# A gate's row moved from the last product's sum on VectorE into that product's weights on GpSimd, in a hybrid attention and Fourier block

## The chip, the core and the metric

The kernel runs on 1 core of one Trainium2 chip. The profile calls the core's engines PE (TensorE, matrix products; PEld are its weight loads), DVE (VectorE), ACT (ScalarE), POOL (GpSimd) and SP (SyncE, which here only issues DMAs). A queue's name ends in q, so SPq and POOLq are DMAs issued by SP and by POOL. The metric is the device time of one execution in microseconds (us). Before the change the median of 3 runs is 1297.37 us (1297.19 to 1297.37).

## The reference, cut to what matters

One layer for 512 tokens with 2048 channels. The end of it is all that the change touches:

```python
def _merge(p_rest, attn, w_pa, w_pb, w_o):
    ...
    return (g_a * y_a + g_b * y_b) @ w_o          # 512 x 2048 by 2048 x 2048

    shift, scale, gate = jnp.split(silu_c @ w_ada[l] + b_ada[l], 3, axis=-1)
    ...
    y = _merge(p[..., OFF_ZA:], attn, w_proj_a[l], w_proj_b[l], w_out[l])
    new_xs = xs + gate[:, None] * y               # gate: one value for each channel
    ...
    return _rmsnorm(xs, final_g)                  # over the 2048 channels of a token
```

`gate` depends on the condition alone, so it is one row of 2048 numbers. A product's column c is multiplied by gate[c], which is the same as a product with weights whose column c was multiplied by gate[c] beforehand.

## The kernel before, in words

All products are f32, worked out as three fp32r products each: a factor is split into a high part (ACT copies it rounded, L179) and a low part (DVE subtracts, L180), and PE sums high*high, high*low and low*high (L335, L336, L337). Tiles `whi`, `wlo` and, in turn with them, pairs named `s` hold the split weights; a raw weight tile has 128 partitions x 1024 (two blocks of 128 rows by 512 columns) and is named `wr` (loaded by SP) or `R` (see below).

The large products are done by a scheme of seven half-size products in place of eight (Strassen and Winograd). A group is a product of 512 tokens by 2048 channels with 1024 output columns, of which two groups, 8 and 9, make the output projection `w_o`. In group 9, the last one of the kernel, the seven products run in the order P1, Q5, P2, Q6, P7, Q3, Q4. Each has 4 weight pieces and 48 matmuls. Products with a letter Q take weights that are sums of blocks of `w_o`: four tiles `R` (in this text the chain), one for each piece, are added to by DMAs from POOL (L288). For P7, DVE subtracts a freshly loaded block from the chain's tile to get P7's weights (L273), and then the last block is added to the chain, which gives Q4's weights. Q4's four pieces are split straight from the four tiles `R`.

The sums of the seven products lie in PSUM (`banks`) and are joined by DVE into tiles `X`, `V` and `Y` (L1085), each 2 x 512 columns for 128 tokens at a time. A finished quarter (its half of the tokens, and one of four ranges of 512 columns) is multiplied by the gate's row on DVE (L1839), and x is added to it by a DMA from POOL that accumulates in SBUF (L1841). In the last group this is turned round to save work at the end:

- `prepare` (L1803) forms x - gate*X before product P7 and x - gate*Y before product Q3, by one DVE instruction (L1806) and one accumulating DMA (L1807) each.
- Q4 is summed on in the same PSUM banks as P7, so that the banks hold P7+Q4 at the end. `finish` (L1136) runs Q4 for the first 128 of the half's tokens over all pieces (t = 0), then for the second 128 (t = 1), and calls `last` after each.
- `last` (L1886) multiplies the banks by the gate's row (L1894), adds that to x - gate*Y in two halves of 256 columns (L1896), sums the squares (ACT, L1791), and scales the four quarters of those tokens by the root mean square and the final row (L1879, L1881, L1867), each followed by its store (L1845, L1868).
- Before it, `out_done` for the quarter (0, 1), called when Q3 is done (L1809), does the same with L1814 and L1815 for the first half of the tokens, in an order on DVE and ACT that is written out by hand.

The order of the rest is set by a recording scheduler: `get` (L294) splits weights ahead of their use, as far as there are tiles for them, and in group 9 the split of a piece follows the split before it. A tile's readers wait by semaphores for its writers. Each engine's instructions, and the DMA issues among them, run in the order in which they stand.

`split_piece` (L261) is the place at which a weight piece is split. The rows of the gate lie in SBUF as `gates[0]` and `gates[1]` of 128 x 1024 each, the same values in all partitions, loaded by POOL (L1744).

Of the kernel before, what the change touches and what calls it, by code (L numbers as in the profile page):

```python
# [13 lines left out]
ALU = mybir.AluOpType  # L14
# [4 lines left out]
P = 128  # L19
# [52 lines left out]
def context_piece(g, name, pc):  # L72

    n = 28 * (g - NQZ) + 4 * ONE_GROUP.index(name) + pc
    if n % 2 == 0 and 0 <= n < 8:
        return "cn", n // 2
    if n % 7 == 4 and 18 <= n < 46:
        return "cr", n // 7 - 2
# [43 lines left out]
def block_kernel(ctx, tc, xT, ctx_rows, ctx_toks, x, c_row, w_ss, w_gate, vecs, qkg, rope, dft_c, dft_s,  # L122
                 w_start, w_g, w_pab, w_o, final_g, out):
    nc = tc.nc
# [30 lines left out]
    def uid(s):  # L155
        cnt[0] += 1
        return f"{s}{cnt[0]}"
# [20 lines left out]
    def split_from(src, hi, lo):  # L178
        first = nc.scalar.activation(hi, src, ACT.Copy)  # L179
        return first, nc.vector.tensor_tensor(lo, src, hi.bitcast(F32), op=ALU.subtract)  # L180
# [58 lines left out]
    def int_tiles(n):  # L239
        return [Halves([pairs[2 * n + k][i][:, :, 256:] for k in range(2)]) for i in range(2)]  # L240

    def hl_tiles():
        if more_hl and not more_hl[0]:
            hl_pools.extend(range(MORE_HL))
            more_hl.clear()
        elif more_hl:
            more_hl[0] -= 1
        hl_pools.append(hl_pools.pop(0))
        pool = hl_pools[-1]
        if isinstance(pool, tuple):  # L250
            return [slot_tile(p, (1024,), F32R) for p in pool]
        if isinstance(pool, int):
            return int_tiles(pool)
        return [pool.tile([P, 1024], F32R, tag=t, bufs=hl_pools.count(pool), name=uid("w" + t)) for t in ("hi", "lo")]
# [2 lines left out]
    last_split, split_of, in_line = [], [], []  # L257

    look = [1]

    def split_piece(e):  # L261
        if e.out is not None or e.kind == "raw":
            return
        raws = [r for _, r in e.raws]
        src = raws.pop(0) if e.stage is None else chain[e.pc]
        for r in raws:
            nc.vector.tensor_tensor(src, src, r, op=ALU.add)
        if e.off:
            with ExitStack() as line:
                if e.key[1] in DIFF_IN_LINE:  # L270

                    line.enter_context(tc.issue_after(split_of[-2][1].ins))
                nc.vector.tensor_tensor(src, chain[e.pc], src, op=ALU.subtract)  # L273
        hi, lo = e.dst() if e.dst else hl_tiles()
        if isinstance(hi, Halves):
            for k in range(2):
                last_split.append(split_from(src[:, 512 * k : 512 * k + 512].rearrange("p (a c) -> p a c", a=2),
                                             hi.parts[k], lo.parts[k]))
        else:
            hi, lo = hi[:, : e.cols], lo[:, : e.cols]  # L280
            with ExitStack() as line:
                if in_line:
                    for i in last_split[-1]:
                        line.enter_context(tc.issue_after(i.ins))
                last_split.append(split_from(src, hi, lo))
        split_of.append(last_split[-1])
        if e.nxt is not None:
            nc.gpsimd.dma_start(chain[e.pc], e.nxt, accum_op=ALU.add)  # L288
        if e.stage == 3:
            left[e.pc] = 0  # L290
        r = lambda t: t if isinstance(t, Halves) else t.rearrange("p (n m) -> p n m", n=e.n)
        e.out = (r(hi), r(lo))

    def get(key):  # L294
        load_more()
        turn = [e for e in ahead if not e.aside]
        assert turn[0].key == key, (turn[0].key, key)
        for e in turn[: min(look[0], len(hl_pools))]:
            if e is turn[0] or e.key[0] != "V":
                split_piece(e)  # L300
        load_more()
        e = turn[0]
        ahead.remove(e)
        free.extend(p[0::2] for p, _ in e.raws if p in retired)
        return e.raws[0][1] if e.kind == "raw" else e.out
# [14 lines left out]
    def slot_tile(p, shape, dt):  # L320
        return p[0].tile([P] + list(shape), dt, tag=p[1], bufs=1, name=uid("s"))

    def take(shape, dt=F32, pool=None):
        p = next((p for p in free if p[0] is pool), free[0])
        free.remove(p)
        t = slot_tile(p, shape, dt)
        home[id(t)] = p, t
        return t
# [89 lines left out]
    for g in range(LAST + 1):  # L418
        for name in ONE_GROUP:
# [6 lines left out]
            for pc in range(4):  # L426
                p = context_piece(g, name, pc)
                if p:
                    src, cols = (ctx_toks[p[1]], 1024) if p[0] == "cn" else (ctx_rows[p[1]], 4 * C)
                    stream(p, src, cols, 1, "raw")  # L430
                    todo.insert(len(todo) - 4 + pc, todo.pop())
            for pc in range(4):
                if (g, name, pc) in GATE_AT:
                    q = GATE_AT[g, name, pc]
                    stream(("gate", q), w_gate[q], 1024, 1, "raw")
                    e = todo.pop()
# [286 lines left out]
    def split_next():  # L723
        e = next(e for e in ahead if e.out is None and e.kind != "raw")
        split_piece(e)
        e.raws = []
# [27 lines left out]
    with tc.manual_schedule(engines={E.PE}):  # L754
# [6 lines left out]
        with tc.manual_schedule(engines={E.Activation, E.DVE}):  # L761
# [25 lines left out]
            for kb in range(1, 4):  # L787
                k = kb + 1
# [32 lines left out]
            for kb in range(4, KK - 4, 2):  # L821
# [6 lines left out]
                k = kb + 2  # L828
# [104 lines left out]
    for g in range(4):  # L933
        gate_b(g)
        positions(g)
        if g < 2:
            channels(g + 2)
        with behind((finals[-1], low[g])):
            for e in ahead[:g]:
                split_piece(e)  # L940
# [66 lines left out]
    def job():  # L1007
        tick[0] += 1
        due = next((x for x in later if x[0] <= tick[0]), None)
        if due:  # L1010
            later.remove(due)
            due[1]()
        elif jobs:
            jobs.pop(0)()
# [10 lines left out]
    class Group:  # L1025
# [110 lines left out]
        def finish(self, a, form):  # L1136

            w = []
            for t in range(2):
                for j in range(8):  # L1140
                    if len(w) <= j // 2:
                        w.append(get(("Q4", self.g, j // 2)))
                        job()
                        job()
                    self.mm(a, form, j, t, w[j // 2], False, j == 7, cont=True)
                self.last(self.Y, a, t)

    def gate_done(half, c, v, t):
# [498 lines left out]
    for i in range(NSTEP + 3):  # L1647
        h, t = divmod(i, 4)
# [29 lines left out]
        if i == 3:  # L1678
            with tc.issue_after(maxima[0].ins), tc.issue_after(maxima[1].ins):
                e = take((1024,))  # L1680
# [58 lines left out]
    gates, fgs = {}, {}  # L1739

    def load_rows(g):
        for l, src in ((gates, gs.rearrange("(o k) p -> o (k p)", o=1)), (fgs, final_g)):
            l[g] = take((2, 512))
            nc.gpsimd.dma_start(l[g], src[:, 1024 * g : 1024 * g + 1024].broadcast_to([P, 1024]))  # L1744
# [42 lines left out]
    new_o = lambda: take((2, 512))  # L1787
    squared = take((1024,))

    def squares_of(v, t, i):  # L1790
        nc.scalar.activation(squared[:, : v.shape[-1]], v, ACT.Square, accum_out=ssq[:, t, i : i + 1])  # L1791
# [8 lines left out]
            if j > 1:  # L1800
                nc.vector.tensor_tensor(t, t, row(fgs, j), op=ALU.mult)

    def prepare(t, half, j):  # L1803

        o[half, j] = t
        nc.vector.scalar_tensor_tensor(t, t, -1.0, row(gates, j), op0=ALU.mult, op1=ALU.mult)  # L1806
        nc.gpsimd.dma_start(t, x[half, j], accum_op=ALU.add)  # L1807

# [77 lines left out]
    def last(Y, a, t):  # L1886

        while jobs:
            job()
        tmp = new_o()[:, 0, :]  # L1890
        half = [(slice(0, 256), 0), (slice(256, 512), 4)]
        r = Rms(2 + t)
        with tc.manual_schedule(engines={mybir.EngineType.DVE, mybir.EngineType.Activation}):
            nc.vector.tensor_tensor(tmp, a[:, t, :], gates[0][:, 0, :], op=ALU.mult)  # L1894
            for c, i in half:
                nc.vector.tensor_tensor(Y[:, t, c], tmp[:, c], Y[:, t, c], op=ALU.add)  # L1896
                squares_of(Y[:, t, c], 2 + t, i)
            if t:

                r.rest()  # L1900
                r.root_of(4)
            else:
                r.add()
                r.root()
            r.turn()
            if t:
                r.scale_part(3, half)
            else:
                r.scale(3, True)
            r.scale(1)  # L1910

            r.scale(2, True, nc.scalar if t else None)
            r.scale(0)

    def free_form(name):
        for h in range(2):
            give(*held.pop((name, h)))
# [6 lines left out]
    for name in OUT_GROUP:  # L1924
        out_group.run(name)

    last_group = Group(9, mf, new_o, out_done, {"a": "x", "b": "y", "c": "x"}, last)
    for name in ONE_GROUP:
        if name == "Q3":

            nc.scalar.activation(mhalf[:, 8:9], ssq[:, 0, 2:3], ACT.Sqrt)
            prepare(last_group.Y, 1, 0)
        elif name == "P7":
            prepare(last_group.X, 0, 1)
        if name in ("P7", "Q3"):

            in_line.append(True)
            hl_pools.insert(0, (free.pop(0), free.pop(0)))
            look[0] += 1
        last_group.run(name)  # L1940
        free_form(next(f for n, f, _, _ in PRODUCTS if n == name))
        if name == "P1":
            load_rows(0)
# [81 lines left out]
```

## Time and profile before

| | |
|---|---|
| median of 3 runs | 1297.37 us (1297.19 to 1297.37) |
| the profiled execution | 1296.21 us |
| its span, from first to last instruction | 1294.4 us |
| mean granted clock of TensorE | 0.995 |
| PE, DVE, ACT, POOL busy | 1277.4, 996.1, 683.9, 168.8 us |

Times inside the profile are counted from the start of the span. In a timeline's row stand the start, the duration, the engine, the line, the operation, the tile written and the tiles read; in square brackets, the idle time of the engine before it and what ended that. Back-to-back instructions of one engine can overlap by some 0.1 us, as the next begins while the last drains. Buffer numbers are left out in profile rows, so that `s` is any of many tiles: X, Y and V of the last groups, x - gate*X, and the split weights of every other piece are all called `s`.

### The profile page before, as it was taken

The numbers are of one execution on the slowest core, as the hardware profiler recorded it, in microseconds if no ns is written. First come the engines' busy times: TensorE is split into PE (matmuls) and PEld (weight loads), VectorE is DVE, ScalarE is ACT, GpSimd is POOL, SyncE is SP. The second block draws the span as 40 slices with busy tenths as digits, with TensorE's granted clock in tenths as the row PEclk, the third lists the DMA queues.
The fourth block names the chain that finished last, engine by engine and source line by source line (L and its number), as shares of the span: only waits on it lengthen the run. The fifth ranks groups of instructions, "written<-read, shape, count | busy, mean of one in ns | idle before, by whom it ended". The sixth has DMA issues, their size and how long they took to land.

```text
span 1294.4 us, 17701 instructions
## 1 busy us (share of the span) xinstructions
PE 1277.4 (99%) x6598; PEld 1051.3 (81%) x6598; DVE 996.1 (77%) x1304; ACT 683.9 (53%) x1076; POOL 168.8 (13%) x222
## 2 busy tenths in 40 slices
PE   8999999999999999999999999999999999999997
PEld 5677988888888888888888888888888888888885
DVE  5667899979778787658687756788898777887776
ACT  5322655545455454443355544666667646464554
POOL 0000011110102111012021010011100211211210
PEclk8999999999999999999999999999999999999999
DMA  9999588888899889977879897578862899998985
GB/s 378 408 368 352 197 225 215 241 228 262 207 314 244 254 281 289 291 196 188 272 206 277 274 233 254 177 239 253 262 186 74 247 247 256 246 207 237 220 202 171
DMA packets 104487, 319.61 MB, mean 247 GB/s; under 512 B 9904, under 2 KB 33072, under 8 KB 100432
## 3 DMA queue, kind: packets, MB, share of 16 engines
q1 hardware_dynamic: 55056, 197.86, 42.2%
q0 software_dynamic: 27024, 98.19, 35.9%
q10 hardware_dynamic: 22320, 22.42, 5.1%
q8 instruction: 52, 0.85, 0.3%
q14 instruction: 35, 0.29, 0.1%
HBM read 283.82 MB, written 34.61 MB: 246 GB/s over the span
## 4 chain that ended last, share of the span: by engine, by line
PE 93%; DVE 2%; DMA 2%; ACT 2%; issue 1%; SPq 0%; ACTq 0%; DVEq 0%
PE banks L335 11%; PE banks L336 10%; PE banks L337 10%; PE x L335 9%; PE x L337 9%; PE x L336 9%; PE y L336 7%; PE y L335 7%; PE y L337 7%; PE banks L1512 2%; PE pd L563 2%; PE pb L335 2%; PE pb L336 2%; PE pb L337 1%; PE pc L335 1%; PE pc L337 1%
## 5 line engine op out<-in xcount | busy, mean ns | idle before, releaser
L179 ACT ACTIVATE whi<-R 128x1024 fp32r<-128x1024 f32 x138 | 145.4, 1058 | 143.2 <-PE banks L337 47.6
L180 DVE TENSOR_TENSOR wlo<-R,whi 128x1024 fp32r<-128x1024 f32 x138 | 167.5, 1220 | 55.5 <-ACT whi L179 55.3
L180 DVE TENSOR_TENSOR wlo<-wr,whi 128x1024 fp32r<-128x1024 f32 (+1 forms) x122 | 147.1, 1211 | 65.5 <-ACT whi L179 65.4
L179 ACT ACTIVATE whi<-wr 128x1024 fp32r<-128x1024 f32 (+1 forms) x122 | 127.4, 1051 | 126.9 <-PE y L337 41.6
L335 PE MATMUL banks<-whi,s 128*128 128x512 f32 x396 | 157.1, 397 | 1.0 <-DVE ev L1085 1.0
L336 PE MATMUL banks<-wlo,s 128*128 128x512 f32 x396 | 155.2, 392 | 0.0
L337 PE MATMUL banks<-whi,s 128*128 128x512 f32 x396 | 155.0, 391 | 0.0
L335 PE MATMUL x<-whi,s 128*128 128x512 f32 x352 | 137.1, 390 | 0.0
L337 PE MATMUL x<-whi,s 128*128 128x512 f32 x352 | 137.0, 389 | 0.0
L336 PE MATMUL x<-wlo,s 128*128 128x512 f32 x352 | 137.0, 389 | 0.0
L335 PE MATMUL y<-whi,s 128*128 128x512 f32 x316 | 123.0, 389 | 0.6 <-DVE cxe L1235 0.6
L336 PE MATMUL y<-wlo,s 128*128 128x512 f32 x316 | 123.1, 389 | 0.1
L337 PE MATMUL y<-whi,s 128*128 128x512 f32 x316 | 122.8, 389 | 0.0
L288 POOL DMA_DIRECT2D R<-in_w_g x64 | 55.9, 873 | 412.2 <-DVE wlo L180 242.3
L179 ACT ACTIVATE s<-wr 128x512 fp32r<-128x512 f32 (+2 forms) x93 | 60.4, 677 | 70.3 <-DMA wr<-cf_d 23.9
L180 DVE TENSOR_TENSOR s<-wr,s 128x512 fp32r<-128x512 f32 (+2 forms) x93 | 66.8, 747 | 32.9 <-ACT s L179 32.0
L335 PEld LDWEIGHTS banks<-whi,s 128*128 128x128 f32 x396 | 74.4, 188 | 16.8 <-issue 1.4
L337 PEld LDWEIGHTS banks<-whi,s 128*128 128x128 f32 x396 | 74.4, 188 | 15.5
L336 PEld LDWEIGHTS banks<-wlo,s 128*128 128x128 f32 x396 | 74.5, 188 | 14.0 <-DVE wlo L180 0.3
L336 PEld LDWEIGHTS x<-wlo,s 128*128 128x128 f32 x352 | 66.1, 188 | 13.8 <-DVE wlo L180 0.2
L337 PEld LDWEIGHTS x<-whi,s 128*128 128x128 f32 x352 | 66.1, 188 | 13.7
L335 PEld LDWEIGHTS x<-whi,s 128*128 128x128 f32 x352 | 66.1, 188 | 13.6
(321 smaller groups left out, 2826.9 us busy)
## 6 DMA issues: line engine op xcount, KB each, us to landing
wr<-in_w_g SPq DMA_DIRECT2D x128, 512.0 KB, 5.9
R<-in_w_g POOLq DMA_DIRECT2D x64, 512.0 KB, 7.5
wa<-in_w_ss SPq DMA_DIRECT2D x31, 1024.0 KB, 9.5
R<-in_w_g SPq DMA_DIRECT2D x32, 512.0 KB, 5.9
wr<-in_w_gate SPq DMA_DIRECT2D x32, 512.0 KB, 5.2
wr<-in_w_o SPq DMA_DIRECT2D x24, 512.0 KB, 7.2
R<-in_w_o POOLq DMA_DIRECT2D x24, 512.0 KB, 9.5
wr<-in_w_pab SPq DMA_DIRECT2D x20, 512.0 KB, 5.7
```

The costliest lines, as they stand in the source:

```text
L179: first = nc.scalar.activation(hi, src, ACT.Copy)
L180: return first, nc.vector.tensor_tensor(lo, src, hi.bitcast(F32), op=ALU.subtract)
L288: nc.gpsimd.dma_start(chain[e.pc], e.nxt, accum_op=ALU.add)
L335: nc.tensor.matmul(o, ah, bh, start=start, stop=False, skip_group_check=cont)
L336: nc.tensor.matmul(o, ah, bl, start=False, stop=False, skip_group_check=cont)
L337: nc.tensor.matmul(o, al, bh, start=False, stop=stop, skip_group_check=cont)
L563: nc.tensor.matmul(acc[32 * j : 32 * j + 32], c2[:, n, :], w[:, k, :], start=n < 4, stop=n >= KK - 4)
L1512: nc.tensor.transpose(tp[:, k * P : (k + 1) * P], p[:, k * P : (k + 1) * P], ident)
```

## The change

The gate's row for Q4 goes into Q4's weights. In `split_piece`, a piece of group 9's Q4 is multiplied in place by the row, by one instruction on POOL (128 x 1024, both inputs in SBUF, the row read twice), before it is split. There are four of them. Q4 then starts its own sum in the banks (it no longer goes on from P7's), and `last` adds the banks straight to x - gate*Y, without L1894.

P7's sum, which Q4 had been added to, is now brought in by `prepare` before Q3: two instructions on DVE (128 x 512 each, one input in PSUM) subtract it from Y, so that x - gate*(Y - P7) is formed.

```diff
@@
     look = [1]
+    by_columns = {}
 
     def split_piece(e):
...
                 nc.vector.tensor_tensor(src, chain[e.pc], src, op=ALU.subtract)
+        if e.key in by_columns:
+            w = src.rearrange("p (k c) -> p k c", k=2)
+            nc.gpsimd.tensor_tensor(w, w, by_columns[e.key].broadcast_to([P, 2, 512]), op=ALU.mult)
         hi, lo = e.dst() if e.dst else hl_tiles()
...
-                    self.mm(a, form, j, t, w[j // 2], False, j == 7, cont=True)
+                    self.mm(a, form, j, t, w[j // 2], j == 0, j == 7)
                 self.last(self.Y, a, t)
...
-    def prepare(t, half, j):
+    def prepare(t, half, j, inner=None):
 
         o[half, j] = t
+        if inner is not None:
+            for i in range(2):
+                nc.vector.tensor_tensor(t[:, i, :], t[:, i, :], inner[:, i, :], op=ALU.subtract)
         nc.vector.scalar_tensor_tensor(t, t, -1.0, row(gates, j), op0=ALU.mult, op1=ALU.mult)
         nc.gpsimd.dma_start(t, x[half, j], accum_op=ALU.add)
...
-        tmp = new_o()[:, 0, :]
         half = [(slice(0, 256), 0), (slice(256, 512), 4)]
         r = Rms(2 + t)
         with tc.manual_schedule(engines={mybir.EngineType.DVE, mybir.EngineType.Activation}):
-            nc.vector.tensor_tensor(tmp, a[:, t, :], gates[0][:, 0, :], op=ALU.mult)
             for c, i in half:
-                nc.vector.tensor_tensor(Y[:, t, c], tmp[:, c], Y[:, t, c], op=ALU.add)
+                nc.vector.tensor_tensor(Y[:, t, c], a[:, t, c], Y[:, t, c], op=ALU.add)
                 squares_of(Y[:, t, c], 2 + t, i)
...
-            prepare(last_group.Y, 1, 0)
+            prepare(last_group.Y, 1, 0, last_group.acc["c"])
+            by_columns.update({("Q4", 9, pc): gates[0][:, 0, None, :] for pc in range(4)})
```

The added lines move the line numbers of what follows: L288 becomes L292, L1085 L1089, L1806 and L1807 become L1813 and L1814, L1839 and L1841 become L1846 and L1848, L1896 becomes L1901. New are L277 (the product on POOL) and L1812 (the subtraction from Y).

On POOL, at the end of the program, the rows before are these. R is the chain with its four tiles; s_10277 is the quarter that P2 finished, s_10129 is x - gate*X, s_10205 is x - gate*Y, and s_10356 is V.

```order
L288 DMA R_1331<-in_w_o 128x1024
L1841 DMA s_10277<-in_x 128x1024
L288 DMA R_1332<-in_w_o 128x1024
L288 DMA R_1329<-in_w_o 128x1024
L288 DMA R_1330<-in_w_o 128x1024
L1807 DMA s_10129<-in_x 128x1024
L1807 DMA s_10205<-in_x 128x1024
L1841 DMA s_10356<-in_x 128x1024
```

Of the same place with the change, s_10131 being the gate's row:

```order
L292 DMA R_1331<-in_w_o 128x1024
L1848 DMA s_10277<-in_x 128x1024
L292 DMA R_1332<-in_w_o 128x1024
L277 TENSOR_TENSOR R_1331<-R_1331,s_10131 128x1024
L292 DMA R_1329<-in_w_o 128x1024
L277 TENSOR_TENSOR R_1332<-R_1332,s_10131 128x1024
L292 DMA R_1330<-in_w_o 128x1024
L277 TENSOR_TENSOR R_1329<-R_1329,s_10131 128x1024
L277 TENSOR_TENSOR R_1330<-R_1330,s_10131 128x1024
L1814 DMA s_10129<-in_x 128x1024
L1848 DMA s_10356<-in_x 128x1024
L1814 DMA s_10205<-in_x 128x1024
```

The four products stand between and behind the last three DMAs of the chain, and the last three DMAs that add x now stand behind all four.

On DVE, around P7's end and the splits of Q4's weights, the rows before are these (banks is P7's sum where L1085 reads it):

```order
L1085 TENSOR_TENSOR s_10205<-s_10356,s_10205 128x1024
L1806 SCALAR_TENSOR_TENSOR s_10129<-s_10129,s_10131 128x1024
L180 TENSOR_TENSOR wlo_10386<-wr_10318,whi_10385 128x1024
L1806 SCALAR_TENSOR_TENSOR s_10205<-s_10205,s_10131 128x1024
L180 TENSOR_TENSOR s_10406<-wr_10383,s_10405 128x1024
L180 TENSOR_TENSOR wlo_10422<-wr_10403,whi_10421 128x1024
L1085 TENSOR_TENSOR s_10356<-s_10356,banks 128x512 x2
L180 TENSOR_TENSOR s_10445<-R_1331,s_10444 128x1024
L1839 TENSOR_TENSOR s_10356<-s_10356,s_10131 128x1024
L180 TENSOR_TENSOR s_10449<-R_1332,s_10448 128x1024
L180 TENSOR_TENSOR wlo_10465<-R_1329,whi_10464 128x1024
L180 TENSOR_TENSOR wlo_10481<-R_1330,whi_10480 128x1024
```

And with the change, from the same row on:

```order
L1813 SCALAR_TENSOR_TENSOR s_10129<-s_10129,s_10131 128x1024
L180 TENSOR_TENSOR wlo_10386<-wr_10318,whi_10385 128x1024
L180 TENSOR_TENSOR s_10406<-wr_10383,s_10405 128x1024
L180 TENSOR_TENSOR wlo_10422<-wr_10403,whi_10421 128x1024
L1089 TENSOR_TENSOR s_10356<-s_10356,banks 128x512 x2
L1812 TENSOR_TENSOR s_10205<-s_10205,banks 128x512
L1846 TENSOR_TENSOR s_10356<-s_10356,s_10131 128x1024
L1812 TENSOR_TENSOR s_10205<-s_10205,banks 128x512
L180 TENSOR_TENSOR s_10448<-R_1331,s_10447 128x1024
L1813 SCALAR_TENSOR_TENSOR s_10205<-s_10205,s_10131 128x1024
L180 TENSOR_TENSOR s_10453<-R_1332,s_10452 128x1024
L180 TENSOR_TENSOR wlo_10470<-R_1329,whi_10469 128x1024
```

The two subtractions of P7's sum stand ahead of the splits of Q4's weights, and the multiplication of Y by the gate's row has moved in among them.

## The prediction

> **What bounds the kernel now.** I read the page's busy times and chain of waits first, then the chain in order of time at its end, then the timelines of DVE, ACT and POOL over the last 50 us.
>
> ```profile
> PE 1277.4 (99%) x6598; PEld 1051.3 (81%) x6598; DVE 996.1 (77%) x1304; ACT 683.9 (53%) x1076; POOL 168.8 (13%) x222
> PE 93%; DVE 2%; DMA 2%; ACT 2%; issue 1%; SPq 0%; ACTq 0%; DVEq 0%
> ```
>
> TensorE is the bound until its last matmul. The change takes no matmul away, so it can win only behind the last one, and lose wherever it makes PE or that end late. DVE from P7's end on:
>
> ```profile
> 1250.61 1.22 DVE L180 TENSOR_TENSOR wlo<-wr,whi 128x1024 fp32r<-128x1024 f32 x1 [0.36 <-ACT whi L179]
> 1251.75 1.22 DVE L180 TENSOR_TENSOR s<-wr,s 128x1024 fp32r<-128x1024 f32 x1
> ...
> 1261.52 1.23 DVE L180 TENSOR_TENSOR wlo<-wr,whi 128x1024 fp32r<-128x1024 f32 x1 [0.61 <-ACT whi L179]
> 1262.66 1.28 DVE L1085 TENSOR_TENSOR s<-s,banks 128x512 f32<-128x512 f32 x2
> ...
> 1269.70 1.23 DVE L180 TENSOR_TENSOR wlo<-R,whi 128x1024 fp32r<-128x1024 f32 x1 [1.23 <-ACT whi L179]
> 1273.37 0.69 DVE L1814 TENSOR_TENSOR s<-banks,s 128x512 f32<-128x512 f32 x1 [2.44 <-PE banks L337]
> 1274.10 0.69 DVE L1815 TENSOR_TENSOR s<-s,s 128x512 f32<-128x512 f32 x1
> ...
> 1282.33 0.16 DVE L1854 TENSOR_REDUCE r<-ssq 128x1 f32<-128x5 f32 x1 [1.24 <-ACT s L1791]
> ...
> 1285.14 0.69 DVE L1894 TENSOR_TENSOR s<-banks,s 128x512 f32<-128x512 f32 x1 [0.68 <-PE banks L337]
> 1285.87 0.76 DVE L1896 TENSOR_TENSOR s<-s,s 128x256 f32<-128x256 f32 x2
> ```
>
> L1814 waits for Q3's last matmul, and L1894 at 1285.14 for Q4's; between them DVE is full but for 1.24 us and 0.68 us. From 1249 to 1273.37 DVE stands idle for 0.36 + 0.61 + 1.23 + 2.44 = 4.64 us, and otherwise issues a 128x1024 instruction every 1.14 us (1251.75 less 1250.61). That 4.64 us is the cover for everything that the change adds there. Nearly all of those instructions read two tiles in SBUF (L180, L273, L1806, L1839); only L1085 from `banks` reads one.
>
> **The gain at the end.** L1894 goes. For the second tokens (t = 1) L1896's successor reads the banks itself, so it can start at 1285.14 in place of 1285.87: 0.73 us off the chain. Reading PSUM in place of SBUF I cost at nothing: at 128x512 both kinds last 0.69 (L1814, L1815). For t = 0 the same 0.73 us buys nothing, since DVE then waits 1.24 us at 1282.33 for ACT's squares. Were nothing else changed, the sum is -0.73 us.
>
> **The two subtractions.** By L1085's pair (1.28 for two, so 0.6 each between starts) they cost DVE 1.2 us ahead of Q4's splits. L1806 for Y only changes its place. Q4's first matmul now overwrites the banks, so it also waits for the second subtraction; that stands ahead of the first split, on which Q4 waits anyway.
>
> **The four products on POOL.** No row has a large one, so I bound it. POOL's rows are these; the last three show a TENSOR_TENSOR of 8 elements that raises to a power:
>
> ```profile
> 0.73 0.21 POOL masks.py:197 MEMSET ident<- 128x128 f32 x1 [0.29 <-POOLq L2017]
> 0.87 0.53 POOL L530 MEMSET s<- 128x512 f32 x1
> 1.44 0.28 POOL masks.py:199 TENSOR_SCALAR_AFFINE_SELECT ident<-ident 128x128 f32<-128x128 f32 x1
> ...
> 204.12 1.67 POOL L1166 TENSOR_TENSOR small<-small,mhalf 128x8 f32<-128x8 f32 x1
> ...
> 204.63 0.68 DVE L973 TENSOR_TENSOR ev<-ev,s 128x512 f32<-128x512 f32 x1
> ```
>
> Writing alone goes at (0.53 - 0.21)/384 = 0.84 ns an element with 0.1 us ahead, so 0.96 us for 1024 is the lower end. The select reads one tile and writes one; less the same 0.1 us it takes 1.46 ns an element, and twice that for two inputs, 3.1 us, is the upper end. Plain scaling of the select by 8 gives 2.25 us, which I take: it is the one row that reads and writes a tile, and lies in the middle. The power's time per element is not used, as a product is no power. The Trainium skill, "GPSIMD Engine Reference", section 3.1, has 4497 ns for an addition of 2048 f32; halved, as an estimate, that is 2.25 us, and the sum would be the same. No run here shows it.
>
> Its own time is not all that a product costs, because POOL and DVE get in each other's way:
>
> ```profile
> 323.45 0.20 POOL L1165 TENSOR_SCALAR small<-small 128x8 f32<-128x8 f32 x1
> ...
> 390.22 1.08 POOL L1165 TENSOR_SCALAR small<-small 128x2 f32<-128x2 f32 x1 [31.35 <-DVE small L1280]
> 391.38 1.56 POOL L1166 TENSOR_TENSOR small<-small,mhalf 128x2 f32<-128x2 f32 x1
> ...
> 390.02 1.23 DVE L267 TENSOR_TENSOR R<-R,wr 128x1024 f32<-128x1024 f32 x1
> 391.17 1.22 DVE L180 TENSOR_TENSOR wlo<-R,whi 128x1024 fp32r<-128x1024 f32 x1
> 392.42 1.22 DVE L267 TENSOR_TENSOR R<-R,wr 128x1024 f32<-128x1024 f32 x1
> ```
>
> The small L1165 takes 0.20 us; at 390.22 it takes 1.08 and ends at 391.30, just behind the end (391.25) of a DVE instruction with two SBUF inputs. L1166 at 391.38, of only 2 elements, likewise outlasts L180 (end 392.39) by 0.5 us. So POOL's read waits until such a DVE instruction is done, then gets its turn: the L267 behind starts 1.25 us after L180 in place of 1.14. I take it that DVE is held off in the same way while POOL reads, here for all of a product, since its reading goes on to its end. Four products then hold DVE for 4 x 2.25 = 9.0 us (3.8 to 12.4 by the bounds). A hold that falls on the PSUM-reading instructions (L1085's pair, the two subtractions) costs nothing there, up to 1.8 us for one of the four.
>
> A rule of the Trainium skill goes further: "SBUF — State Buffer", section "Who interferes with whom", has a GpSimd instruction and a DVE instruction with two SBUF inputs exclude each other for the whole instruction. Here L973, whose two inputs lie in SBUF, ran its usual 0.68 us in the middle of POOL's 1.67 us at 204.12, so this trace does not agree for an instruction that has read its few elements; by the rule the four would cost the same 9.0 us.
>
> **POOL's queue.** What stands behind the waiting products are DMAs:
>
> ```profile
> 1242.57 0.85 POOL L288 DMA_DIRECT2D R<-in_w_o  x1 [18.74 <-ACT whi L179]
> ...
> 1245.97 0.85 POOL L288 DMA_DIRECT2D R<-in_w_o  x1 [1.65 <-ACT whi L179]
> 1248.24 0.85 POOL L288 DMA_DIRECT2D R<-in_w_o  x1 [1.42 <-ACT s L179]
> 1250.78 0.86 POOL L288 DMA_DIRECT2D R<-in_w_o  x1 [1.69 <-ACT whi L179]
> 1257.80 0.86 POOL L1807 DMA_DIRECT2D s<-in_x  x1 [6.16 <-DVE s L1806]
> 1260.07 0.88 POOL L1807 DMA_DIRECT2D s<-in_x  x1 [1.41 <-DVE s L1806]
> 1266.90 0.87 POOL L1841 DMA_DIRECT2D s<-in_x  x1 [5.95 <-DVE s L1839]
> ...
> DMA to landing us min/median/max: 5.8/11.2/11.9
> R<-in_w_o POOLq DMA_DIRECT2D x1, 512.0 KB, 10.4
> s<-in_x POOLq DMA_DIRECT2D x1, 512.0 KB, 7.3
> s<-in_x POOLq DMA_DIRECT2D x1, 512.0 KB, 5.6
> ```
>
> The chain's first tile lands 5.8 us after its issue, at 1248.4; the second (issued at 1245.97) 10.4 after, at 1256.4. Product 1 thus runs at 1249.1 to 1251.4 once the DVE instruction under way is done; the third tile's DMA follows at 1251.4 (now 1248.24), product 2 at 1257.2 to 1259.5, the fourth tile's DMA at 1259.5 (now 1250.78), product 3 at 1260.6 to 1262.9, and product 4, once that DMA lands 5.8 to 7.5 us on, at 1266 to 1269.6. The x for X is then added by a DMA issued at 1268.6 to 1269.7 in place of 1257.80 and lands by 1277.2 at the latest; L1815 wants it at 1274.10. The others follow 1 to 3 us later each, ahead of their use behind 1280.
>
> **The sum.** L1814 stands behind the last split on DVE, so it starts late by X = 9.0 + 1.2 - 4.64 = 5.6 us, or 3.8 if product 4 falls on the PSUM readers; I take 4.6. The x of X (3.1 late at most) lies within that, and so does Q4, whose first matmul runs from 1273.85 now and would wait some 1 us for its splits.
>
> ```profile
> 1273.85 0.39 PE L335 MATMUL banks<-s,s 128*128 128x512 f32 x1
> ```
>
> From 1273.37 on DVE and ACT are a fixed sequence with one idle gap that can close, the 0.68 us at 1285.14. So the end moves by 4.6 - 0.68 - 0.73 = +3.2 us. The profiled execution's 1296.21 becomes 1299.4; the median stands 1.16 above that execution, so 1297.37 + 3.2 = 1300.6 us.
>
> **Rivals.**
> - *No exclusion (not slower).* POOL and DVE run side by side; for it speaks L973's undisturbed 0.68, against it the rows at 390. DVE has 4.64 us for 1.2, and only POOL's queue counts: product 4 ends at 1266.8 to 1268.5, x lands at 1272.6 to 1276.0, between no delay and 1.9 us for L1815. The end moves by -0.73 to +0.5: 1296.6 to 1297.9, taken as 1296.7. It decides once a hold costs DVE under 1.2 us, since X must stay below 1.4 us.
> - *DVE wins every turn.* As its instructions stand back to back, POOL would get in only where DVE idles: 1250.3, then near 1262, 1266 and 1274. The x DMA goes out at 1276.6 and lands 5.6 to 7.5 later, 8 to 10 us behind 1274.10; the end moves by about +6.9 to +8.6: 1305. Against it speaks the turn that POOL got at 392.4.
> - *A product at its upper end.* 12.4 us of holds make X 9.0, and Q4's splits about 4 us late for PE, which the sequence behind hides: +7.6, 1305.
>
> **How the numbers follow.** The forecast's mechanism has 0.50, and its own range from holds and landings is +1 to +5 us (1298.4 to 1302.4); no exclusion 0.30; DVE wins 0.13; the upper end 0.07. From 1296.4 to 1304.9 takes in the first two and the near edges of the rest. About 0.2%, 2.6 us, is what a measurement of this kernel can tell from no change. The forecast passes it for two thirds of its chance, both last cases do: 0.53 slower. All of no exclusion and a third of the forecast's lie within it: 0.45. No part can win more than 0.73 us, so faster keeps 0.02.
>
> **What would show it.** In the profile after: POOL's four L277 at 2.25 us or more; DVE's instructions beside them starting some 2 us late (else no exclusion holds); L1821, the successor of L1814, at about 1278 in place of 1273.37, behind the last split and not behind a DMA (behind x's landing, DVE wins its turns); the add for t = 1 directly behind t = 0's last scaling with no wait for PE. Wrong would make it a product well under 1.2 us, or x landing so late that it, not the holds, sets the end.

## The result and the profile after

The changed kernel takes 1301.1 us (median of 7 runs, 1298.2 to 1301.85), the kernel before 1296.77 us (7 runs, the three shown earlier among them, 1295.28 to 1297.37). The ratio is 1.0026, with a 95% interval of 1.0014 to 1.0038: slower, by 4.3 us between the medians. The prediction was 1300.6 us in a range of 1296.4 to 1304.9, with 0.53 for slower. The profiled execution took 1301.85 us; its span is 1300.0 us.

The page's busy times and the shares of its chain of waits:

```profile
PE 1278.6 (98%) x6598; PEld 1051.0 (81%) x6598; DVE 1004.9 (77%) x1304; ACT 683.8 (53%) x1076; POOL 181.7 (14%) x226
PE 87%; DMA 5%; DVE 2%; issue 2%; ACT 2%; POOL 1%; SPq 0%; ACTq 0%; POOLq 0%; DVEq 0%
```

PE's work is what it was. DVE is busy 8.8 us longer (996.1 before) for the same 1304 instructions, and POOL has four instructions more. POOL's timeline of the last 50 us, with the four products on L277:

```profile
1244.48 0.85 POOL L292 DMA_DIRECT2D R<-in_w_o  x1 [18.74 <-ACT whi L179]
...
1250.06 3.24 POOL L277 TENSOR_TENSOR R<-R,s 128x1024 f32<-128x1024 f32 x1 [1.32 <-DMA R<-in_w_o]
...
1258.45 2.81 POOL L277 TENSOR_TENSOR R<-R,s 128x1024 f32<-128x1024 f32 x1 [4.33 <-DMA R<-in_w_o]
...
1262.31 3.44 POOL L277 TENSOR_TENSOR R<-R,s 128x1024 f32<-128x1024 f32 x1 [0.23 <-DMA R<-in_w_o]
1266.74 3.48 POOL L277 TENSOR_TENSOR R<-R,s 128x1024 f32<-128x1024 f32 x1 [0.99 <-DMA R<-in_w_o]
1270.17 0.87 POOL L1814 DMA_DIRECT2D s<-in_x  x1
```

DVE over the same time and to the end:

```profile
1250.94 3.43 DVE L274 TENSOR_TENSOR wr<-R,wr 128x1024 f32<-128x1024 f32 x1
...
1258.91 3.43 DVE L1089 TENSOR_TENSOR s<-s,s 128x1024 f32<-128x1024 f32 x1
1262.27 1.21 DVE L1813 SCALAR_TENSOR_TENSOR s<-s,s 128x1024 f32<-128x1024 f32 x1
1263.40 3.43 DVE L180 TENSOR_TENSOR wlo<-wr,whi 128x1024 fp32r<-128x1024 f32 x1
...
1267.89 3.42 DVE L180 TENSOR_TENSOR wlo<-wr,whi 128x1024 fp32r<-128x1024 f32 x1
1271.23 1.27 DVE L1089 TENSOR_TENSOR s<-s,banks 128x512 f32<-128x512 f32 x2
...
1278.16 2.35 DVE L180 TENSOR_TENSOR wlo<-R,whi 128x1024 fp32r<-128x1024 f32 x2
1280.44 0.68 DVE L1821 TENSOR_TENSOR s<-banks,s 128x512 f32<-128x512 f32 x1
...
1290.10 1.41 DVE L1886 SCALAR_TENSOR_TENSOR s<-s,r,s 128x512 f32<-128x512 f32 x2
1291.43 0.75 DVE L1901 TENSOR_TENSOR s<-banks,s 128x256 f32<-128x256 f32 x2
```

Beside each product one DVE instruction with two SBUF inputs takes 3.43 us (once 3.42) where its like take 1.22. I call the 2.21 us more a hold. Take the third product: POOL asks at 1262.31, while L1813 runs; L1813 ends at 1263.48; the product ends at 1265.75, 2.27 us later; and the split that began at 1263.40 ends at 1266.83. Four holds of 2.21 us make 8.84 us, and that is the 8.8 us by which DVE's busy time grew. The DVE gap of 2.44 us ahead of L1814, the old name of L1821, is gone: L1821 now stands directly behind the last split. From 1250.94 to 1280.44 DVE's timeline shows no idle time at all, so in this stretch DVE never stood idle for a DMA or for a weight tile.

**A measure for the rest of this text.** The early part of the program, which no edit touches, varies by up to 2.4 us: POOL issues the chain's first weights at 1242.57 before, at 1244.48 after, and at 1242.08 in a second profile of the changed kernel. So I use the stretch from that issue to the issue of the last store on ACT, which is the last row of ACT's timeline. After:

```profile
1295.10 0.34 ACTq L1852 DMA_DIRECT2D out_y<-s  x1
```

And before:

```profile
1289.54 0.34 ACTq L1845 DMA_DIRECT2D out_y<-s  x1
```

Before, the stretch lasts 1289.54 - 1242.57 = 46.97 us; after, 1295.10 - 1244.48 = 50.62 us. The change costs 3.65 us in the stretch that it touches (predicted: 3.2). The spans differ by 5.6 us, of which 1.9 us is the later start.

### The profile page after: what moved, and what is told of

It reads as the page before. It is cut to its first block, busy times and chain, and to the rows that moved or that the text cites. A ratio compares the mean times of both kernels' runs of the same rounds, so it can differ in the third digit from the quotient of the medians.

```text
span 1300.0 us, 17710 instructions
## 1 busy us (share of the span) xinstructions
PE 1278.6 (98%) x6598; PEld 1051.0 (81%) x6598; DVE 1004.9 (77%) x1304; ACT 683.8 (53%) x1076; POOL 181.7 (14%) x226
## 4 chain that ended last, share of the span: by engine, by line
PE 87%; DMA 5%; DVE 2%; issue 2%; ACT 2%; POOL 1%; SPq 0%; ACTq 0%; POOLq 0%; DVEq 0%
PE x L340 9%; PE x L339 9%; PE x L341 9%; PE banks L339 8%; PE banks L340 8%; PE banks L341 8%; PE y L339 7%; PE y L340 7%; PE y L341 7%; PE banks L1516 2%; PE pd L567 2%; PE pb L339 1%; PE pb L340 1%; PE pb L341 1%; DMA s<-yb_d 1%
## 5 line engine op out<-in xcount | busy, mean ns | idle before, releaser
L180 DVE TENSOR_TENSOR wlo<-R,whi 128x1024 fp32r<-128x1024 f32 x138 | 167.5, 1221 | 52.6 <-ACT whi L179 52.5
L180 DVE TENSOR_TENSOR wlo<-wr,whi 128x1024 fp32r<-128x1024 f32 (+1 forms) x122 | 151.6, 1248 | 63.3 <-ACT whi L179 63.1
L292 POOL DMA_DIRECT2D R<-in_w_g x64 | 55.9, 874 | 412.4 <-DVE wlo L180 241.5
L180 DVE TENSOR_TENSOR s<-wr,s 128x512 fp32r<-128x512 f32 (+2 forms) x93 | 66.9, 749 | 35.3 <-ACT s L179 34.6
```

## The experiments

The theory was that POOL's reading holds off DVE's instructions with two SBUF inputs. The rivals were that POOL's queue (the products ahead of the DMAs) makes the cost; that the two subtractions or the other parts of the change do; or that the products would be as dear anywhere. All edits below are made to the changed kernel. "Stretch" is the difference to the 46.97 us of before in one profile each; ratios are of whole times to the kernel before, with the 95% interval.

| kernel | stretch, us | whole, us (runs) | ratio to before |
|---|---|---|---|
| the change | +3.65 | 1301.1 (7) | 1.0026, 1.0014 to 1.0038 |
| e1_no_product | -0.72 | 1296.04 (11) | 0.9993, 0.9984 to 1.0002 |
| e2_write_only | -0.72 | 1295.91 (11) | 0.9992, 0.9983 to 1.0001 |
| e3_on_dve | -0.41 | 1296.34 (11) | 0.9996, 0.9987 to 1.0005 |
| e4_one_read | -0.72 | 1295.76 (11) | 0.9992, 0.9984 to 1.0001 |
| e5_p7_alone | +0.01 | 1296.32 (10) | 0.9996, 0.9987 to 1.0005 |
| e6_dve_y_from_v | -0.56 | 1295.85 (11) | 0.9992, 0.9983 to 1.0001 |
| e7_pool_y_from_v | +1.26 | 1299.18 (10) | 1.0017, 1.0008 to 1.0026 |
| e9_two_two | -0.43 | 1296.38 (10) | 0.9995, 0.9986 to 1.0004 |
| a2_again | +3.68 | 1299.39 (1) | - |
| e11_two_two_again | +0.18 | 1297.29 (1) | - |
| e10_last_two | -0.72 | 1297.39 (1) | - |

The kernel before took 1297.06 us beside e1 to e4, 1297.04 us beside e5 to e9 (33 runs each), and 1296.72 us beside the last three.

**Without the products (e1_no_product).**

```diff
-        if e.key in by_columns:
-            w = src.rearrange("p (k c) -> p k c", k=2)
-            nc.gpsimd.tensor_tensor(w, w, by_columns[e.key].broadcast_to([P, 2, 512]), op=ALU.mult)
```

> The changed kernel without the four products on GpSimd; Q4's weights stay unscaled, so the gate is left out of Q4's part. All theories agree on a control: with no products VectorE has 4.64 us of idle time for the 1.2 us of subtractions, the add for the last tokens starts 0.73 us earlier, so 0.7 us less than before (ratio 0.9994). If it stays some 3 us above before, neither the products nor their waits are the cause, but the joined sum of P7.

The stretch is 0.72 us shorter than before. So all of the loss comes with the four products, and the gain at the end is there once they are gone: 0.73 us had been worked out for it.

**POOL writes the same tiles and reads nothing (e2_write_only).**

```diff
-            w = src.rearrange("p (k c) -> p k c", k=2)
-            nc.gpsimd.tensor_tensor(w, w, by_columns[e.key].broadcast_to([P, 2, 512]), op=ALU.mult)
+            for _ in range(3):
+                nc.gpsimd.memset(src, 0.01)
```

> In place of each product GpSimd overwrites the same weight tile three times with a constant (the gate and the weights are left out of Q4): about 2.9 us of GpSimd per piece, behind the same landing and ahead of the same split, but nothing is read from SBUF. Exclusion by reading: VectorE's instructions keep 1.22 us, and the end comes 0.7 us before to 0.5 us after that of the kernel before. Queue theory (the delay comes from the DMAs that stand behind the products on GpSimd): as slow as the change, 3 to 4 us above before.

The group of the writes by line, with shortest, mean and longest in ns, then rows of the POOL and DVE timelines:

```profile
L277 POOL MEMSET R<- x12: 944/955/1433, 1249.0 to 1268.8; 128x1024 f32 x12
```

```profile
1261.46 4.53 POOL L277 MEMSET R<- 128x1024 f32 x5 [2.84 <-DMA R<-in_w_o]
1265.94 0.87 POOL L1814 DMA_DIRECT2D s<-in_x  x1
```

```profile
1257.03 1.22 DVE L1813 SCALAR_TENSOR_TENSOR s<-s,s 128x1024 f32<-128x1024 f32 x1
...
1274.11 0.69 DVE L1821 TENSOR_TENSOR s<-banks,s 128x512 f32<-128x512 f32 x1 [0.91 <-PE banks L341]
```

POOL is busy for about 12 x 0.955 = 11.5 us, longer than the four products' 9.1 us without their waits, yet DVE keeps to 1.22 us, L1821 waits for PE again, and the stretch is -0.72 us. The Trainium skill, "SBUF — State Buffer", section "Who interferes with whom", says that a DVE instruction with two SBUF inputs contends with a GpSimd instruction that reads SBUF and not with one that only writes; by these rows the trace agrees. POOL being occupied is not what costs. The queue is tested less hard than meant, because the program's scheduler put x's DMA ahead of the last three writes: it goes out at 1265.94, which is 22.63 us into the stretch, against 25.69 us after the change.

**The products on DVE (e3_on_dve).**

```diff
-            nc.gpsimd.tensor_tensor(w, w, by_columns[e.key].broadcast_to([P, 2, 512]), op=ALU.mult)
+            nc.vector.tensor_tensor(w, w, by_columns[e.key].broadcast_to([P, 2, 512]), op=ALU.mult)
```

> The four products on VectorE, all else as changed. Exclusion: each costs VectorE 1.14 us in place of a hold of 2.2, together 4.56 + 1.2 against 4.64 us of cover, so its chain starts 1.1 to 1.4 us late, of which 0.7 fits into the gap before Q4's end: 0.3 us below before to level with it. Load theory (any work of VectorE in this stretch costs its full time at the end): 5.8 - 0.7, so about 5 us above before.

The products by line (ns again), and the DVE rows behind Q3:

```profile
L277 DVE TENSOR_TENSOR R<-R,s x4: 1217/1221/1227, 1248.4 to 1272.6; 128x1024 f32<-128x1024 f32 x4
```

```profile
1273.75 0.68 DVE L1821 TENSOR_TENSOR s<-banks,s 128x512 f32<-128x512 f32 x1
...
1275.08 1.22 DVE L180 TENSOR_TENSOR wlo<-R,whi 128x1024 fp32r<-128x1024 f32 x1
```

On DVE a product takes one turn of 1.14 us; on POOL it took 2.21 us of DVE's time. The whole computation in this form is 0.41 us shorter than before in the stretch. The fourth split has gone behind L1821 here, so the order is not quite that of the change. With it ahead, L1821 would start 1.14 us later, and by the sum under "The end" below I estimate the stretch at about 0.1 us below before.

**One tile read in place of two (e4_one_read)** (scaled by 0.5 in place; the gate is left out of Q4).

```diff
-            w = src.rearrange("p (k c) -> p k c", k=2)
-            nc.gpsimd.tensor_tensor(w, w, by_columns[e.key].broadcast_to([P, 2, 512]), op=ALU.mult)
+            nc.gpsimd.tensor_scalar(src, src, 0.5, None, op0=ALU.mult)
```

> Each product replaced by a multiplication by a constant on GpSimd, which reads one tile in place of two (the gate is left out of Q4). Exclusion for as long as GpSimd reads: holds of 1.1 to 1.5 us each in place of 2.2, so VectorE's chain starts 1 to 2.6 us late and the end lies between 0.4 us below and 1.2 us above before. Exclusion only of two-input instructions: no holds, 0.7 us below before.

POOL's first of the four, and DVE's instructions, with the four that run beside them (2.06, 2.06, 2.62 and 1.78 us):

```profile
1247.59 3.47 POOL L276 TENSOR_SCALAR R<-R 128x1024 f32<-128x1024 f32 x1 [1.46 <-DMA R<-in_w_o]
```

```profile
1247.19 1.22 DVE L180 TENSOR_TENSOR s<-wr,s 128x1024 fp32r<-128x1024 f32 x1 [0.18 <-ACT s L179]
1248.34 2.06 DVE L274 TENSOR_TENSOR wr<-R,wr 128x1024 f32<-128x1024 f32 x1
...
1256.07 2.06 DVE L1812 SCALAR_TENSOR_TENSOR s<-s,s 128x1024 f32<-128x1024 f32 x1
...
1259.19 2.62 DVE L180 TENSOR_TENSOR s<-wr,s 128x1024 fp32r<-128x1024 f32 x1
...
1264.66 1.78 DVE L1845 TENSOR_TENSOR s<-s,s 128x1024 f32<-128x1024 f32 x1
```

The holds are 0.84, 0.84, 1.40 and 0.56 us, 3.64 us together. They were expected at 1.1 to 1.5 us each, which only one of them meets, so the size was missed, and the other answer, no holds, is false too. Why the same instruction holds DVE for 0.56 us once and for 1.40 us another time is open. POOL's own instruction is not shorter for it: the first runs from the end of L180 at 1248.41 to 1251.06, 2.65 us, against 2.27 us for the product. So a hold does not last as long as POOL's instruction; less is read, and less is held. With 3.64 us of holds and 1.2 us of subtractions against a cover of 4.64 us, next to nothing is left over: L1820, the successor of L1814 here, starts 1272.67 - 1241.87 = 30.80 us into the stretch, just as L1814 did before, and the stretch is -0.72 us.

**The subtractions alone (e5_p7_alone)** (no products, and the end as before).

```diff
-        if e.key in by_columns:
...
+        tmp = new_o()[:, 0, :]
...
+            nc.vector.tensor_tensor(tmp, a[:, t, :], gates[0][:, 0, :], op=ALU.mult)
             for c, i in half:
-                nc.vector.tensor_tensor(Y[:, t, c], a[:, t, c], Y[:, t, c], op=ALU.add)
+                nc.vector.tensor_tensor(Y[:, t, c], tmp[:, c], Y[:, t, c], op=ALU.add)
```

> One part alone: P7's sum is subtracted from Y early and Q4 starts its own sum, but Q4's weights stay as they were and the multiplication by the gate's row stays at the end. Cover theory: 1.2 us of subtractions vanish in 4.64 us of idle time, so level with before (within 0.1 us from the chain's first load in this stretch, 46.97 us before, to the last store's issue). Load theory (the subtractions cost at the end): up to 1.2 us more.

The wait of DVE for Q3's last matmul:

```profile
1272.73 0.69 DVE L1818 TENSOR_TENSOR s<-banks,s 128x512 f32<-128x512 f32 x1 [1.17 <-PE banks L338]
```

The gap shrank from 2.44 to 1.17 us, that is by the 1.2 us of the two subtractions, and the stretch moved by +0.01 us. The cover is real: one sees it being used.

**Without the two subtractions** (Y formed from V only after P7's result has been taken from V; the whole computation), with the products on DVE (e6_dve_y_from_v, which also has the edit of e3) and on POOL (e7_pool_y_from_v).

```diff
                 sub(self.V, a, self.X)
...
-                sub(self.Y, self.V, self.Y)
+                if not self.last:
+                    sub(self.Y, self.V, self.Y)
...
                     sub(self.V[:, t, :], self.V[:, t, :], a[:, t, :])
+                if self.last:
+                    sub(self.Y, self.V, self.Y)
...
-            prepare(last_group.Y, 1, 0, last_group.acc["c"])
+            prepare(last_group.Y, 1, 0)
```

> The four products on VectorE and no subtractions: Y is formed from V after P7's sum has been taken from V, which holds P7 already. Sum rule: 4.56 us against 4.64 us of cover, with a wait of up to 1.5 us for the last landing inside; its chain starts 0 to 0.9 us late, so 0.5 to 0.73 us below before (46.25 to 46.5 us in the stretch that takes 46.97).

> The products on GpSimd as in the change, but no subtractions (Y from V after P7). Sum rule: holds of 4 x 2.21 against 4.64 us of cover, chain 4.0 to 4.2 us late, so the stretch of 46.97 us before takes 2.6 to 2.8 us more (3.65 more with the subtractions). If the subtractions had only been hidden behind the holds, it stays at 3.65.

With the products on DVE this is the shortest of the complete kernels, -0.56 us in the stretch; over the whole time, 0.9992 with 1.0 inside the interval, it can't be told from the kernel before. With the products on POOL the stretch is +1.26 us, where +2.6 to +2.8 us was expected. DVE's rows show why:

```profile
1248.81 3.43 DVE L274 TENSOR_TENSOR wr<-R,wr 128x1024 f32<-128x1024 f32 x1
...
1261.27 3.43 DVE L180 TENSOR_TENSOR s<-wr,s 128x1024 fp32r<-128x1024 f32 x1
...
1265.76 1.27 DVE L1089 TENSOR_TENSOR s<-s,banks 128x512 f32<-128x512 f32 x2
1266.95 2.23 DVE L180 TENSOR_TENSOR s<-R,s 128x1024 fp32r<-128x1024 f32 x1
```

And POOL's issue of x's DMA:

```profile
1268.04 0.88 POOL L1817 DMA_DIRECT2D s<-in_x  x1
```

Three holds are whole. The fourth product, which POOL wants from 1264.89 on, falls on the pair that reads `banks`: the pair keeps its 1.27 us, and only the rest of the product, 1.02 us, holds the split behind. That is 1.2 us less than I had counted. This run also speaks against the queue: x's DMA goes out 1268.04 - 1242.35 = 25.69 us into the stretch, exactly as after the change, and yet the stretch is 2.4 us shorter. What it shows of the fourth product is one execution, at 1297.34 us the second fastest of ten; by the medians of whole times the kernel is 2.1 us slower than before (1.0 to 3.4), so the relief need not be there each time.

**Two products on DVE, two on POOL (e9_two_two)**, and the same kernel again (e11_two_two_again).

```diff
-            nc.gpsimd.tensor_tensor(w, w, by_columns[e.key].broadcast_to([P, 2, 512]), op=ALU.mult)
+            (nc.vector if e.key[2] < 2 else nc.gpsimd).tensor_tensor(w, w, by_columns[e.key].broadcast_to([P, 2, 512]), op=ALU.mult)
```

> The change with the first two products on VectorE (1.14 us each) and the last two on GpSimd (holds of 2.21 us each). Sum rule: 2.28 + 4.42 + 1.2 - 4.64 = 3.3 us late, less 1.41, so the stretch of 46.97 us takes 1.9 us more; if a hold falls on instructions that read PSUM, down to 0. Queue theory: the chain's loads are no longer held up, and the last loads of x by 5 us less, so 0.7 us less than before.

> The kernel with two products on each engine once more. There the third product waited from 1259.57 to 1262.93 while VectorE ran two instructions with two SBUF inputs unhindered. If that order of turns is set by the program, the third product lasts 5.6 us again; if it is chance, VectorE is held off at once and the third lasts 2.8 to 3.4 us.

The first execution, POOL and then DVE:

```profile
1259.57 5.63 POOL L277 TENSOR_TENSOR R<-R,s 128x1024 f32<-128x1024 f32 x1 [6.60 <-DMA R<-in_w_o]
```

```profile
1259.44 1.22 DVE L180 TENSOR_TENSOR s<-wr,s 128x1024 fp32r<-128x1024 f32 x1
1260.57 1.21 DVE L277 TENSOR_TENSOR R<-R,s 128x1024 f32<-128x1024 f32 x1
1261.71 1.22 DVE L180 TENSOR_TENSOR wlo<-wr,whi 128x1024 fp32r<-128x1024 f32 x1
1262.85 1.27 DVE L1089 TENSOR_TENSOR s<-s,banks 128x512 f32<-128x512 f32 x2
...
1264.64 1.64 DVE L1846 TENSOR_TENSOR s<-s,s 128x1024 f32<-128x1024 f32 x1
...
1266.80 2.82 DVE L180 TENSOR_TENSOR s<-R,s 128x1024 fp32r<-128x1024 f32 x1
```

And the second, POOL and then DVE:

```profile
1261.73 3.49 POOL L277 TENSOR_TENSOR R<-R,s 128x1024 f32<-128x1024 f32 x1 [7.60 <-DMA R<-in_w_o]
```

```profile
1261.73 1.22 DVE L277 TENSOR_TENSOR R<-R,s 128x1024 f32<-128x1024 f32 x1
...
1263.02 3.28 DVE L180 TENSOR_TENSOR wlo<-wr,whi 128x1024 fp32r<-128x1024 f32 x1
```

In the first, POOL's record begins at 1259.57, and yet DVE starts two more instructions with two SBUF inputs, at 1260.57 and 1261.71, which run at their usual 1.21 and 1.22 us; POOL's product comes to its end only beside and behind the pair that reads `banks`. The holds are 0.42 and 1.60 us, the stretch -0.43 us, where about +1.9 us was expected; the whole times of the ten runs, at most 0.5 us above before by their interval, exclude +1.9 us too. In the second execution of the same program POOL's record begins at 1261.73, at the same time as DVE's own product, and POOL gets its turn right behind it: its product lasts 3.49 us and not 5.6, the split is held for 2.06 us, and the stretch is +0.18 us. So the two executions differ already in when POOL asks, and only the first has DVE instructions that start well after POOL and are served ahead of it. It is enough to say that the turn does not always go to POOL at the next boundary between two DVE instructions. What decides it is open.

**The change once more (a2_again).**

> The changed kernel once more, for its trace. Holding theory: four VectorE instructions of some 3.4 us beside the four products again, and 50.6 us from the chain's first load to the last store's issue. If turns at the shared reading are a matter of chance, some of the four run at 1.22 us and the product waits longer.

The stretch is 50.65 us (+3.68). The first two of its four held DVE instructions:

```profile
1248.54 3.43 DVE L274 TENSOR_TENSOR wr<-R,wr 128x1024 f32<-128x1024 f32 x1
...
1257.65 3.42 DVE L1813 SCALAR_TENSOR_TENSOR s<-s,s 128x1024 f32<-128x1024 f32 x1
```

The other two take 3.44 and 3.45 us. In this order of work POOL had its turn all eight times that were seen.

**The last two products alone (e10_last_two)** (the gate is missing from Q4's first two pieces).

```diff
-            nc.gpsimd.tensor_tensor(w, w, by_columns[e.key].broadcast_to([P, 2, 512]), op=ALU.mult)
+            if e.key[2] >= 2:
+                nc.gpsimd.tensor_tensor(w, w, by_columns[e.key].broadcast_to([P, 2, 512]), op=ALU.mult)
```

> Only the last two products, on GpSimd; the first two are left out, so the gate is missing from half of Q4's weights. If it was VectorE's own product that passed ahead of GpSimd's, the third is now served at the next boundary (2.8 to 3.4 us) and holds one VectorE instruction for 2.2 us; if VectorE simply keeps its turn there, it lasts until the first instruction that reads PSUM.

This was to tell whether the two products that DVE did in the run above had decided the turn. It doesn't:

```profile
1263.34 1.85 DVE L180 TENSOR_TENSOR wlo<-wr,whi 128x1024 fp32r<-128x1024 f32 x1 [1.49 <-ACT whi L179]
```

DVE stood idle for 1.49 us ahead of this split, and the product did most of its reading there; only 0.63 us was held, so nobody had to give way, and the question stays open.

## Why the prediction was right

- **PE as the bound, and the gain at the end.** Right. Without the products the stretch is 0.72 us shorter, against 0.73 us worked out. After the change L1901 at 1291.43 stands directly behind t = 0's scaling with no wait for PE, as was to be seen.
- **The two subtractions at 1.2 us, hidden.** Right: 1.27 us for the pair, and with them alone the gap ahead of L1818 shrank by 1.27 us at no cost.
- **The product's own time, 2.25 us from the select's row.** Right: 2.27 us once POOL has its turn. The way to it has luck in it: the figure is 8 times a 128-element select that reads one tile, and the one-input scaling of e4, which reads one tile too, took 2.65 us beside a busy DVE. The bounds of 0.96 and 3.1 us, from writing and from twice the select, were wider than needed; the rival at the upper end is out.
- **The hold.** The prediction took the two rows at 390 us, where an instruction of POOL's on two elements delays DVE by 0.1 us, to mean a hold of 4 x 2.25 = 9.0 us. Measured: 4 x 2.21 = 8.84 us. For a product with two inputs the hold is thus as long as the product, as was assumed; for one with a single input (e4) it is not. The sign that was to be looked for, DVE instructions that start some 2 us late, shows as records that start in their place and last 2.21 us longer. "No exclusion" is out by the 3.43 us rows: the same instructions keep 1.22 us where POOL only writes.
- **Who gets the turn.** "DVE wins every turn" did not happen in the change, eight times out of eight. It did for a while in the kernel with two products on each engine.
- **The delay X of L1821.** This is the mis-sized term. X was taken at 4.6 us, between 5.6 and 3.8, allowing for a fourth product on the PSUM readers. In the trace L1821 starts 1280.44 - 1244.48 = 35.96 us into the stretch and L1814 before 1273.37 - 1242.57 = 30.80 us, so X = 5.16 us. The fourth product fell on a split (3.42 us at 1267.89) and was held in full, ahead of the pair at 1271.23; the relief that had been allowed for came only where Y was formed from V. The ledger 8.84 + 1.2 - 4.64 = 5.4 us is 0.24 us above X, because the cover was counted some 0.3 us too small. The idle times in brackets begin at the end of an instruction, but an instruction that lasts 1.22 us is followed after 1.14 us when nothing is waited for; each of the four gaps hides another 0.08 us. With 4.97 us of cover the ledger gives 5.07 us.
- **The end, X - 0.68 - 0.73.** Right in form. With X = 5.16 this is 3.75 us, and 3.65 us was measured; the closed gap of 0.68 us, taken from start to start as above, is worth 0.76 us, which gives 3.67 us. The prediction's 3.2 us is short by X alone. The sum X - 0.76 - 0.73 holds for the other kernels with a delay beyond that gap as well: X is 2.77 us in e7, 0.94 us in e6 and 1.69 us in e11, which gives +1.28, -0.55 and +0.20 us, where +1.26, -0.56 and +0.18 us were measured.
- **The queue.** Right that it would not limit. The issue of x's DMA, at 1270.17, is 25.69 us into the stretch; before, L1807's was 15.23 us in, and the prediction's 1268.6 to 1269.7 means 26.0 to 27.1 us. It landed with room to spare, as the chain in order of time and DVE's timeline have it:

```profile
1270.17 5.47 DMA s<-in_x
```

```profile
1281.15 0.69 DVE L1822 TENSOR_TENSOR s<-s,s 128x512 f32<-128x512 f32 x1
```

It lands at 1275.64, which is 31.16 us into the stretch, and L1822 needs it at 1281.15. Even L1815 before, at 1274.10 and so 31.53 us into the stretch, would have found it landed. The chain does run through POOL and this DMA (POOL's share is 1%, DMA's 5%); that alone would have misled.
- **Q4's first matmul**, said to wait some 1 us:

```profile
1275.76 0.39 PE L339 MATMUL banks<-s,s 128*128 128x512 f32 x1
...
1278.30 0.50 PE L340 MATMUL banks<-s,s 128*128 128x512 f32 x1 [0.62 <-DVE s L180]
```

It starts 31.28 us into the stretch, as before (1273.85 - 1242.57 = 31.28); PE stands for 0.62 us later on, waiting for a split. It is hidden, as the prediction had it.

**The number.** The predicted 1300.6 us is 0.5 us under the median. That closeness has some luck in it: the prediction added 3.2 us to a median of 1297.37 us, while all seven runs of before have a median of 1296.77 us, a difference of 4.3 us. Of that the stretch explains 3.65 us; the rest is inside the interval of the ratio (1.8 to 4.9 us of 1296.77). One sum of a rival is off: an x that lands 8 to 10 us late moves the end, less the 0.68 and 0.73 us, by +6.6 to +8.6 us and not from +6.9 on, which changes neither its 1305 nor the forecast.

## What to carry to other kernels

Before an elementwise operation is moved from VectorE to GpSimd, look at what VectorE does at that time: beside instructions that read two SBUF tiles, a two-input product on GpSimd cost VectorE 2.21 us, while the same product on VectorE itself costs a turn of 1.14 us. In these runs it took nothing from VectorE only where VectorE was idle or read from PSUM, or where GpSimd merely wrote (0.955 us a tile, no hold). Add up the idle time of the held engine up to the next wait that it must meet, 4.64 us here by the brackets and 4.97 us from start to start: as long as holds and added work stay below it nothing is lost. What lies above comes out at the end, less the later gaps that it closes (0.76 us here).

## What the runs showed of the hardware that I had not expected

- **The hold goes with the reading, not with the length of GpSimd's instruction.** A product with two inputs lasts 2.27 us and held DVE for 2.21 us; a scaling with one input lasts 2.65 us and held it for 0.56 to 1.40 us. Writing 12 tiles held it not at all.
- **The turn is not fixed.** In the change's order POOL had its turn eight times out of eight, but one execution of the kernel with two products on each engine let POOL wait past two DVE instructions that started 1.0 and 2.1 us after it. The Trainium skill, "SBUF — State Buffer", section "Who interferes with whom", says that the order of issue decides who blocks; the row at 1259.57 beside those at 1260.57 and 1261.71 does not agree with that for these instructions, if the order of the recorded starts is the order of issue.
